# Probabilities handed to fp32r tiles by DMA before their transposes, a new order inside a stream step, and branch projections chained to the stream's fill

## The chip, the cores and the metric

The kernel runs on one core of a Trainium2 chip (trn2). The metric is the device time of one execution in microseconds. The kernel before takes 1494.45 us, the median of three runs (1493.89 to 1494.85).

## The reference

One encoder layer is applied to two groups of requests with the same weights: `prompt` (1024 tokens) and `sample` (512 tokens), both 1024 wide, each with 256 memory tokens.

```
h = rms_norm(x, ln_pre);  z = h @ w_in            # split into nine fields
pool_out  = multiscale_pool(pool_in) * pool_scale
attn_out  = softmax(q k^T / 8) v                  # 8 query heads, 2 key heads, rotary q and k
cross_out = softmax(xq mk^T / sqrt(128)) mv       # 4 heads, 256 memory tokens
branches  = (pool_out * silu(pool_gate), attn_out * silu(attn_gate), cross_out * silu(x_gate))
merged    = sum_n sigmoid(merge_logits_n + b_n) * (branches[n] @ w_branch[n])
y         = x + rms_norm(merged @ w_out, ln_post)
```

Everything is fp32.

## The kernel before

**Arithmetic.** TensorE works on fp32r tiles. Where a product needs more precision, an operand is split into a high part (a copy by ScalarE, line 165) and a low part (a subtraction by VectorE, line 162), and `mm3` (line 132) makes three products of one. All matrix products are recorded at line 126 (`mm`), all transposes at line 130 (`tr`); so one looks at tiles, not lines, to tell them apart. A transpose takes `ident` (fp32) or `identr` (fp32r) as its second operand; in the profile these show as `A<-ident,u` and `B<-identr,u`.

**Tiles.** In SBUF: `u` (128 x 1024, 7 buffers), `med` (128 x 2048, 14), `hu` (128 x 512, 8), `raw` (weights as loaded, 3), `whi`/`wlo` (split weights, 2 each). In PSUM: `A` (two tiles of two banks) and `B` (four tiles of one bank). Intermediate fields go to DRAM scratch and come back (`q`, `xq`, `x_gate`, `attn_gate`, `merge`, `br0` to `br2`). All DMAs are issued by SyncE (SP).

**Stages.** The memory keys and values and the normalised prompt; the prompt's input products (`products`, a scheme with seven products for eight); the first of the sample's input products; then the *stream*; then the branch projections and output products of the three blocks of 512 tokens.

**The stream (lines 888 to 897).** It runs 92 units: 64 of prompt self-attention (`attention`: one 128-token block and one head each), 4 + 4 of prompt cross-attention (`cross`), 16 of sample self-attention (`pairs_of`) and 4 of sample cross-attention. A unit has four parts:

- `ahead`: loads queries two steps early.
- `scores`: query by key products into an `A` tile; VectorE reduces the row maximum (line 782), ScalarE takes the exponential out of PSUM into a `u` tile p (line 784), VectorE the reciprocal of the sum, GpSimd scales p (line 786). Lines 844 to 851 and 927 to 935 are the same for pairs and cross units.
- `turn`: eight 128 x 128 transposes of p into another `A` tile; ScalarE and VectorE split it into `med` tiles.
- `values`: products of the values with the turned probabilities into a `B` tile; `gated` (line 874) or the end of `cross` multiplies by the gate and stores to `br1` or `br2`.

Step i of the stream emits scores of unit i, turn of unit i - 2 (`LAG`), values of unit i - 4 (`LAG + VLAG`). After each of these three parts it yields an amount of TensorE time, and `weave` (line 108) spends that on the *fill*: the rest of the sample's input products (`plain`, 16 pairs of weight tiles), in pieces of twelve products. The price of a product in this planner is its columns over 2.4 ns; of a transpose 107 ns with `ident` and 56 with `identr`, which counts only for transposes in the fill. A unit owes 2560 (cross: 3410) x `SHARE` 0.66 ns per step. Where the fill is spent, the stream goes on alone. After the stream comes what is left of the fill, then `branches(0, sc, merged)`: for three branches, load (`from_scratch`), split, and eight products of twelve matmuls each (`merge`, line 981).

The program order is only a priority: the compiler's scheduler places each engine's instructions in a fixed order by priority and by when their operands and buffers are expected, so an instruction can be pulled ahead. `tc.high_priority` raises some (reductions, splits, evacuations). Engines then run their orders strictly, and wait by semaphore.

Of the kernel before, what the change touches and what calls it, by code (L numbers as in the profile page):

```python
# [61 lines left out]
def encoder_kernel(ctx: ExitStack, tc, wt, xs, xts, mt, cols, rows, rope, edge, ys):  # L62
# [41 lines left out]
    def run(g):  # L104
        for _ in g:
            pass
# [641 lines left out]
    def from_scratch(field, bs, dt=F32):  # L748
# [3 lines left out]
            load(t[:, c * BLK:(c + 1) * BLK], field[c][:, bs])  # L752
        return t

    def attention(b, sc, kt, vt):

        bs = slice(b * BLK, (b + 1) * BLK)
        qd, gd, out = sc["q"], sc["attn_gate"], sc["br1"]
        nch = KC
        units = [(jp, hd, j) for jp in range(TT // 2) for hd in range(NH) for j in range(2)]  # L760
        state = {}

        def ahead(i):
            jp, hd, j = units[i]
            if hd == 0 and j == 0:
                t = M()
                for x in range(2):
                    load(t[:, x * D:(x + 1) * D].bitcast(F32), qd[b * TT + jp * 2 + x][:])
                state["q", jp] = t

        def scores(i):
            jp, hd, j = units[i]
            g = hd // (NH // NG)
            q = state["q", jp][:, j * D + hd * P:j * D + (hd + 1) * P]
            a = A()
            for n in range(2):
                ns = slice(n * 512, n * 512 + 512)
                mm(a[:, ns], q, kt[g][0][:, ns], start=True, stop=False)
                mm(a[:, ns], q, kt[g][1][:, ns], start=False, stop=True)
            mx, sm, rc = S(1), S(1), S(1)  # L780
            with tc.high_priority(PMAX):
                v.reduce_max(mx[:], a[:], axis=AX.X, negate=True)  # L782
                p = U()
                act.activation(p, a[:], AF.Exp, bias=mx[:], accum_out=sm[:])  # L784
            v.reciprocal(rc[:], sm[:])  # L785
            pool.tensor_scalar(p, p, rc[:], 1.0, op0=ALU.mult, op1=ALU.mult)  # L786
            state[i] = p

        def turn(i):
            jp, hd, j = units[i]  # L790
            p = state.pop(i)
            if j == 0:
                state["pt", i // 2] = M()[:], M()[:]
            pv = [t.rearrange("p (c j n) -> p c j n", c=nch, j=2) for t in state["pt", i // 2]]
            tp = A()
            for c in range(nch):
                tr(tp[:, c * P:(c + 1) * P], p[:, c * P:(c + 1) * P], ident)
            tv = tp[:].rearrange("p (c n) -> p c n", c=nch)
            with tc.high_priority(PTURN):
                split(pv[0][:, :, j], pv[1][:, :, j], tv)  # L800

        def values(i):

            jp, hd, j = units[i]
            g = hd // (NH // NG)
            if j == 0:
                state["o"] = B()
            o, pts = state["o"], state["pt", i // 2]
            for c in range(j * nch // 2, (j + 1) * nch // 2):
                for s in range(2):  # L810
                    mm(o[:, :256], vt[:, c, g].rearrange("p s d -> p (s d)"), pts[s][:, c * 256:(c + 1) * 256],
                       start=(c == 0 and s == 0), stop=(c == nch - 1 and s == 1))
            if j == 0:
                return
            del state["pt", i // 2]
            gated(state, jp, hd, o, gd, out, b)

        return [(ahead, scores, turn, values, i, 2560) for i in range(len(units))]

    def pairs_of(sc, kt, vt):  # L820

# [30 lines left out]
            state[i] = p  # L852

        def turn(i):
            p, tp, pt = state[i], A(), M()
            for c in range(4):
                for j in range(2):
                    tr(tp[:, c * 256 + j * P:c * 256 + (j + 1) * P], p[:, j * BLK + c * P:j * BLK + (c + 1) * P], ident)
            with tc.high_priority(PTURN):
                split(pt[:, :D], pt[:, D:], tp[:])  # L860
            state[i] = pt

        def values(i):
# [8 lines left out]
        return [(ahead, scores, turn, values, i, 2560) for i in range(len(units))]  # L872

    def gated(state, jp, hd, o, gd, out, b):
        r = slice((hd % 2) * 64, (hd % 2) * 64 + 64)
        c, cs = hd // 2, slice(b * BLK + jp * 256, b * BLK + jp * 256 + 256)
        if hd % 2 == 0:
            state["ot"] = HU(), HU()
            load(state["ot"][1][:, :256], gd[c][:, cs])
        ot, gt = state["ot"]  # L880
        with tc.high_priority(EVAC):
            act.activation(ot[r, :256], o[64:128, :256], AF.Copy)
            v.tensor_tensor(ot[r, :256], o[0:64, :256], ot[r, :256], op=ALU.add)
        if hd % 2:
            pool.tensor_tensor(ot[:, :256], ot[:, :256], gt[:, :256], op=ALU.mult)
            nc.sync.dma_start(out[c][:, cs], ot[:, :256])

    def stream(units):

        n = len(units)  # L890
        for i in range(-2, n + LAG + VLAG):
            more = units[min(max(i, 0), n - 1)][5] * SHARE / 3
            for k, lag in enumerate((-2, 0, LAG, LAG + VLAG)):
                if 0 <= i - lag < n:
                    units[i - lag][k](units[i - lag][4])
                if k > 0 and i >= 0:
                    yield more

    def cross(b, sc, mkd, mvd):

# [36 lines left out]

        def turn(c):
            p = state[c]
            tp = A()  # L940
            for m in range(2):
                for t in range(TT):
                    tr(tp[:, m * 512 + t * P:m * 512 + (t + 1) * P], p[:, t * 256 + m * P:t * 256 + (m + 1) * P], ident)
            pt = M()
            split(pt[:, 0:1024], pt[:, 1024:2048], tp[:])
            state[c] = pt

        def values(c):
            pt, mv = state.pop(c), state["mv"]
            o = B()  # L950
            for m in range(2):
                s = slice(m * 512 + c * XHD, m * 512 + (c + 1) * XHD)
                mm3(o[:], (mv[0][:, s], mv[1][:, s]), (pt[:, m * 512:(m + 1) * 512], pt[:, 1024 + m * 512:1024 + (m + 1) * 512]), m == 0, m == 1)
            g = HU()
            load(g[:], gd[c][:, bs])
            with tc.high_priority(EVAC):
                v.tensor_tensor(g[:], o[:], g[:], op=ALU.mult)
            nc.sync.dma_start(out[c][:, bs], g[:])

        return [(ahead, scores, turn, values, c, 3410) for c in range(NXH)]  # L960

    def branch_parts(field, bs):
        t = from_scratch(field, bs)
# [153 lines left out]

LAG, VLAG, SHARE, LOOK, WAIT = 2, 2, 0.66, 1, 6  # L1120

AHEAD, EVAC, PMAX, PTURN, LATER = 120, 200, 150, 150, 200

# [89 lines left out]
```

## Time and profile before

The profiled execution took 1496.65 us; the span from first to last instruction is 1494.8 us, and the rest lies around it. Times of stages are windows of that span.

| stage | window, us | length | PE busy | ScalarE busy | clock | DMA share |
|---|---|---|---|---|---|---|
| memory, normalisation | 0 to 75 | 75 | 63.00 | 39.42 | 0.95 | 0.67 |
| prompt input products | 75 to 660 | 585 | 577.24 | 264.42 | 0.99 | 0.34 |
| sample input products, first part | 660 to 692 | 32 | 31.43 | 10.94 | 1.00 | 0.44 |
| stream with the fill | 692 to 1157 | 465 | 453.43 | 288.03 | 0.99 | 0.38 |
| branches, first prompt block | 1157 to 1225 | 68 | 68.00 | 20.26 | 0.97 | 0.71 |
| the other blocks and outputs | 1225 to 1495 | 270 | 262.91 | 86.50 | 1.00 | 0.57 |

PE is TensorE's products, PEld its weight loads (which overlap the products), DVE VectorE, ACT ScalarE, POOL GpSimd, SP SyncE. A row of a group gives line, engine, operation, tile out and tiles in, shapes, the count, then busy time in us and mean ns of one, then the idle time before them and what ended it. A row of the timeline gives start, length, engine, line and operation; "x8" means eight instructions merged, and a bracket is idle time before it with its releaser. Products of TensorE are pipelined and the recorded ends are modelled, so the distance between starts is the cost of one, not its length. A row of the stage view gives window, length, then busy time with count of PE, PEld, DVE, ACT and POOL, then the granted clock, the share of the DMA engines' time and GB/s.

### The profile page before, as it was taken

What the parts mean: (1) busy time and instruction counts of PE and PEld (TensorE: products, weight loads), DVE (VectorE), ACT (ScalarE), POOL (GpSimd) and SP (SyncE); (2) the same over time, 40 slices, a digit from 0 to 9 for tenths busy, and PEclk for the clock granted to TensorE, in tenths of its full rate; (3) what the DMA queues carried; (4) which work ended last, traced back from release to release, by engine and by line L of the source; (5) the groups of instructions that cost most, each with busy time, mean ns of one, the idle gap of its engine ahead of it and who ended that gap; (6) DMA issues with size and microseconds to landing.
All of it is one profiled execution on the core that took longest, in us unless ns stands there. A gap on an engine that the chain in (4) does not pass through costs nothing.

```text
span 1494.8 us, 19564 instructions
## 1 busy us (share of the span) xinstructions
PE 1456.0 (97%) x7264; PEld 1210.1 (81%) x7264; DVE 976.5 (65%) x1215; ACT 709.6 (47%) x1083; POOL 273.3 (18%) x286
## 2 busy tenths in 40 slices
PE   7979999999999999999999999999998999999998
PEld 5768888888888888887888888888886888888887
DVE  6996586666648564747767666676775664764764
ACT  6444444544434545434656556566675233323332
POOL 1000020110000000301222222234232150250241
PEclk9989999999999999999999999999999999999999
DMA  7513233332422434344222223165446844954952
GB/s 277 172 47 106 85 114 125 108 132 66 129 92 78 158 133 128 102 150 148 64 96 80 91 68 106 58 219 173 155 155 214 286 148 132 347 193 140 336 163 84
DMA packets 88174, 211.37 MB, mean 141 GB/s; under 512 B 9872, under 2 KB 19216, under 8 KB 87312
## 3 DMA queue, kind: packets, MB, share of 16 engines
q1 hardware_dynamic: 88080, 210.14, 42.7%
q8 instruction: 57, 0.93, 0.3%
q14 instruction: 37, 0.30, 0.1%
HBM read 155.57 MB, written 54.53 MB: 141 GB/s over the span
## 4 chain that ended last, share of the span: by engine, by line
PE 85%; DMA 4%; DVE 4%; ACT 4%; issue 2%; SPq 1%; POOL 0%; DVEq 0%; POOLq 0%; ACTq 0%
PE B L126 66%; PE A L126 14%; PE A L130 5%; ACT u L784 1%; DVE s L782 1%; ACT whi L165 1%; DMA raw<-wt 1%; DVE wlo L162 1%; PE B L130 1%; DMA hu<-xq 1%; ACT med L165 1%; SPq L139 1%; DMA u<-x_prompt 0%; DMA hu<-merge 0%; DMA hu<-x_gate 0%
## 5 line engine op out<-in xcount | busy, mean ns | idle before, releaser
L126 PE MATMUL B<-med,whi 128*128 128x512 f32 x2776 | 871.2, 394 | 15.8 <-ACT med L165 15.8
L126 PEld LDWEIGHTS B<-med,whi 128*128 128x128 f32 x2776 | 515.8, 189 | 122.2 <-ACT med L165 17.5
L126 PE MATMUL B<-med,wlo 128*128 128x512 f32 x1388 | 544.1, 392 | 0.6 <-DVE wlo L162 0.6
L126 PEld LDWEIGHTS B<-med,wlo 128*128 128x128 f32 x1388 | 261.9, 189 | 56.6 <-DVE wlo L162 1.7
L162 DVE TENSOR_TENSOR wlo<-raw,whi 128x1024 fp32r<-128x1024 f32 (+1 forms) x169 | 213.3, 1263 | 141.6 <-ACT whi L165 140.7
L165 ACT ACTIVATE whi<-raw 128x1024 fp32r<-128x1024 f32 (+1 forms) x169 | 167.5, 991 | 288.5 <-PE B L126 198.3
L165 ACT ACTIVATE med<-A 128x1024 fp32r<-128x1024 f32 x92 | 94.3, 1025 | 108.4 <-PE A L130 108.2
L162 DVE TENSOR_TENSOR med<-A,med 128x1024 fp32r<-128x1024 f32 (+1 forms) x93 | 113.0, 1215 | 42.0 <-ACT med L165 40.8
L187 POOL TENSOR_SCALAR s<-s 128x16 f32<-128x16 f32 (+3 forms) x17 | 6.9, 404 | 669.0 <-DVE s L556 333.2
L786 POOL TENSOR_SCALAR u<-u,s 128x1024 f32<-128x1024 f32 x64 | 72.1, 1127 | 251.3 <-DVE s L785 219.1
L130 PE MATMUL A<-ident,u 128*128 128x128 f32 x784 | 102.8, 273 | 0.9 <-DVE med L162 0.2
L130 PEld LDWEIGHTS A<-ident,u 128*128 128x128 f32 x784 | 90.1, 140 | 16.3 <-issue 5.2
L998 POOL TENSOR_TENSOR med<-med,hu 128x512 f32<-128x512 f32 x48 | 77.0, 1617 | 142.3 <-DVE hu L996 142.2
L782 DVE TENSOR_REDUCE s<-A 128x1 f32<-128x1024 f32 x64 | 78.1, 1220 | 32.9 <-PE A L126 11.3
L126 PE MATMUL A<-kt,med 128*128 128x512 f32 x320 | 91.9, 409 | 2.7 <-ACT u L784 1.2
L126 PE MATMUL A<-whi,med 128*128 128x512 f32 (+1 forms) x320 | 92.4, 368 | 0.2 <-ACT hu L1027 0.2
L784 ACT ACTIVATE u<-A,s 128x1024 f32<-128x1024 f32 x64 | 71.3, 1114 | 38.4 <-DVE s L782 38.0
L165 ACT ACTIVATE whi<-sum 128x1024 fp32r<-128x1024 f32 x50 | 53.1, 1062 | 65.6 <-PE B L126 63.7
L162 DVE TENSOR_TENSOR med<-med,med 128x1024 fp32r<-128x1024 f32 (+1 forms) x50 | 55.8, 1127 | 38.1 <-ACT med L165 34.2
L165 ACT ACTIVATE med<-med 128x1024 fp32r<-128x1024 f32 (+1 forms) x44 | 44.2, 1017 | 74.8 <-POOL med L998 36.2
L162 DVE TENSOR_TENSOR wlo<-sum,whi 128x1024 fp32r<-128x1024 f32 x50 | 61.1, 1221 | 23.3 <-ACT whi L165 22.4
L126 PE MATMUL B<-med,vt 128*128 128x256 f32 x512 | 75.9, 287 | 0.4 <-ACT med L165 0.4
(179 smaller groups left out, 1610.4 us busy)
## 6 DMA issues: line engine op xcount, KB each, us to landing
raw<-wt SPq DMA_DIRECT2D x168, 512.0 KB, 3.7
merge<-hu SPq DMA_DIRECT2D x72, 256.0 KB, 2.0
hu<-merge SPq DMA_DIRECT2D x72, 256.0 KB, 5.2
med<-br SPq DMA_DIRECT2D x36, 256.0 KB, 5.6
q<-hu SPq DMA_DIRECT2D x24, 256.0 KB, 2.6
br<-hu SPq DMA_DIRECT2D x24, 256.0 KB, 2.3
med<-q SPq DMA_DIRECT2D x12, 512.0 KB, 5.0
med<-xt_prompt SPq DMA_DIRECT2D x4, 1024.0 KB, 13.2
```

The source lines that it names most:

```text
L126: pe.matmul(out, l, r, **k)
L130: pe.transpose(out, x, i[:])
L139: return nc.sync.dma_start(out, src)
L162: v.tensor_tensor(out, x, hi.bitcast(F32), op=ALU.subtract)
L165: act.activation(hi, x, AF.Copy)
L187: pool.tensor_scalar(ss, ss, EPS, 1.0, op0=ALU.add, op1=ALU.mult)
L782: v.reduce_max(mx[:], a[:], axis=AX.X, negate=True)
L784: act.activation(p, a[:], AF.Exp, bias=mx[:], accum_out=sm[:])
L786: pool.tensor_scalar(p, p, rc[:], 1.0, op0=ALU.mult, op1=ALU.mult)
L998: pool.tensor_tensor(at, at, sg[:], op=ALU.add)
```

## The change

- A new last part of each unit, `hand`, allocates another `u` tile of type fp32r and copies the scaled probabilities into it by a DMA that ScalarE issues. It runs at the end of the step after the unit's scores.
- `turn` transposes that copy with `identr` into an `A` tile of type fp32r, which is then read as fp32.
- Within a step the order becomes scores, values, turn, hand; `LAG` goes from 2 to 3, so turn comes three steps after the scores, values five.
- The gated outputs of attention and cross units are no longer stored where they are made: they are listed in `finished`, and stored by SP at the end of the following step.
- `branches(0, sc, merged)` is chained to the fill, so that when the sample's input products are spent inside the stream, branch projections follow; what is left of both runs after the stream.

The diff, without the two further `turn` functions (in `pairs_of` and `cross`) that change in the same way:

```
+    def handed(p):
+        t = U(F32R)
+        act.dma_start(t.bitcast(F32), p)
+        return t
+
+    def hand_on(state):
+        def hand(i):
+            state[i] = handed(state[i])
+        return hand
...
-            tp = A()
+            tp = A(F32R)
             for c in range(nch):
-                tr(tp[:, c * P:(c + 1) * P], p[:, c * P:(c + 1) * P], ident)
-            tv = tp[:].rearrange("p (c n) -> p c n", c=nch)
+                tr(tp[:, c * P:(c + 1) * P], p[:, c * P:(c + 1) * P], identr)
+            tv = tp[:].bitcast(F32).rearrange("p (c n) -> p c n", c=nch)
...
-        return [(ahead, scores, turn, values, i, 2560) for i in range(len(units))]
+        return [(ahead, scores, turn, values, hand_on(state), i, 2560) for i in range(len(units))]
...
-            nc.sync.dma_start(out[c][:, cs], ot[:, :256])
+            finished.append((out[c][:, cs], ot[:, :256]))
+
+    finished = []
...
-            more = units[min(max(i, 0), n - 1)][5] * SHARE / 3
-            for k, lag in enumerate((-2, 0, LAG, LAG + VLAG)):
+            more = units[min(max(i, 0), n - 1)][6] * SHARE / 3
+            late = finished[:]
+            finished.clear()
+            for k, lag in ((0, -2), (1, 0), (3, LAG + VLAG), (2, LAG), (4, 1)):
                 if 0 <= i - lag < n:
-                    units[i - lag][k](units[i - lag][4])
-                if k > 0 and i >= 0:
+                    units[i - lag][k](units[i - lag][5])
+                if 0 < k < 4 and i >= 0:
                     yield more
+            for out, x in late:
+                nc.sync.dma_start(out, x)
+        for out, x in finished:
+            nc.sync.dma_start(out, x)
...
-            nc.sync.dma_start(out[c][:, bs], g[:])
-
+            finished.append((out[c][:, bs], g[:]))
...
+    fill = chain(fill, branches(0, sc, merged))
     weave(stream(units), fill)
     run(fill)
-    run(branches(0, sc, merged))
...
-LAG, VLAG, SHARE, LOOK, WAIT = 2, 2, 0.66, 1, 6
+LAG, VLAG, SHARE, LOOK, WAIT = 3, 2, 0.66, 1, 6
```

More of the change, by code (lines that the diff above doesn't have):

```diff
@@ L870, in values @@
             gated(state, jp, hd, o, gd, out, 0)
-        return [(ahead, scores, turn, values, i, 2560) for i in range(len(units))]
+        return [(ahead, scores, turn, values, hand_on(state), i, 2560) for i in range(len(units))]
     def gated(state, jp, hd, o, gd, out, b):
@@ L939, in turn @@
             p = state[c]
-            tp = A()
+            tp = A(F32R)
             for m in range(2):
                 for t in range(TT):
-                    tr(tp[:, m * 512 + t * P:m * 512 + (t + 1) * P], p[:, t * 256 + m * P:t * 256 + (m + 1) * P], ident)
+                    tr(tp[:, m * 512 + t * P:m * 512 + (t + 1) * P], p[:, t * 256 + m * P:t * 256 + (m + 1) * P], identr)
             pt = M()
-            split(pt[:, 0:1024], pt[:, 1024:2048], tp[:])
+            split(pt[:, 0:1024], pt[:, 1024:2048], tp[:].bitcast(F32))
             state[c] = pt
@@ L957, in values @@
                 v.tensor_tensor(g[:], o[:], g[:], op=ALU.mult)
-            nc.sync.dma_start(out[c][:, bs], g[:])
-        return [(ahead, scores, turn, values, c, 3410) for c in range(NXH)]
+            finished.append((out[c][:, bs], g[:]))
+        return [(ahead, scores, turn, values, hand_on(state), c, 3410) for c in range(NXH)]
     def branch_parts(field, bs):
```

6 lines of the change are left out of this document (3 added, 3 removed).

## The prediction

> **What bounds the kernel now.** I read the page first, then the stages, then the PE groups, waits and single rows of the stage that the change touches.
>
> ```profile
> span 1494.8 us, 19564 instructions
> PE 1456.0 (97%) x7264; PEld 1210.1 (81%) x7264; DVE 976.5 (65%) x1215; ACT 709.6 (47%) x1083; POOL 273.3 (18%) x286
> PE 85%; DMA 4%; DVE 4%; ACT 4%; issue 2%; SPq 1%; POOL 0%; DVEq 0%; POOLq 0%; ACTq 0%
> ```
>
> TensorE is busy for 97% of the span and carries 85% of the chain that ended last, so time is won by taking work off TensorE or by filling its holes, and not by making another engine faster. The profiled execution took 1496.65 us (span 1494.8); the median of the runs shown is 1494.45, so I subtract 2.2 us at the end.
>
> The change touches one stage, the stream of attention units, which by the stages (columns: window, length, busy of PE, PEld, DVE, ACT, POOL, clock, DMA share, GB/s) lasts from about 692 to 1157 us:
>
> ```profile
> 805.00:985.00 180.00, 177.56 (x1054) 148.94 (x1053) 118.07 (x143) 107.24 (x155) 49.31 (x47) 1.00 0.29 95
> 1100.00:1144.00 44.00, 43.64 (x279) 38.32 (x278) 31.94 (x42) 34.09 (x77) 18.36 (x30) 1.00 0.60 191
> 1144.00:1157.00 13.00, 5.92 (x26) 4.11 (x23) 6.10 (x7) 2.12 (x3) 0.00 (x0) 0.77 0.93 297
> 692.00:1157.00 465.00, 453.43 (x2680) 384.20 (x2680) 316.88 (x392) 288.03 (x506) 139.77 (x168) 0.99 0.38 123
> ```
>
> There are two kinds of stage in it. Up to 1144 TensorE is full (177.56 of 180). In the last 13 us it does 5.92 us of work, and the granted clock falls to 0.77. Inside the full part the holes are small, and the waits of the weight loads in 692 to 1157 name them (total us, times, longest):
>
> ```profile
> PEld A L126 <- ACT u L784: 11.5, 29, 0.8
> PEld B L126 <- ACT med L165: 8.8, 5, 7.5
> ```
>
> The first is the scores of a unit waiting for a PSUM tile that the exponential of an earlier unit still reads; the second is nearly all the hole at the end (one wait of 7.5).
>
> **Transposes.** 92 units (64 attention, 16 pairs, 12 cross) turn their probabilities with 8 transposes each, 736 in all. They now read fp32; afterwards fp32r. The trace has both forms, since the key and query tails already turn fp32r tiles:
>
> ```profile
> L130 PE MATMUL A<-ident,u 128*128 128x128 f32 x736 | 95.6, 273 | 0.9 <-DVE med L162 0.2
> L130 PE MATMUL B<-identr,u 128*128 128x128 f32 x96 | 11.1, 239 | 0.2 <-DVE u L162 0.2
> ```
>
> ```profile
> 205.09 0.39 PE L126 MATMUL B<-med,wlo 128*128 128x512 f32 x1
> 205.32 0.46 PE L130 MATMUL B<-identr,u 128*128 128x128 f32 x4
> ...
> 206.15 0.40 PE L126 MATMUL B<-med,wlo 128*128 128x512 f32 x1
> 206.38 0.62 PE L126 MATMUL B<-med,whi 128*128 128x512 f32 x2
> 206.84 0.39 PE L126 MATMUL B<-med,wlo 128*128 128x512 f32 x1
> ...
> 623.90 0.80 PE L130 MATMUL B<-identr,med 128*128 128x128 f32 x8
> 624.55 1.06 PE L130 MATMUL A<-ident,med 128*128 128x128 f32 x8
> 625.37 0.71 PE L126 MATMUL B<-med,whi 128*128 128x512 f32 x2
> 625.92 0.40 PE L126 MATMUL B<-med,wlo 128*128 128x512 f32 x1
> ```
>
> Durations overlap, so I price by starts. The fp32 bursts are busy 95.6/92 = 1.039 us each; less the last one's 0.273, over seven gaps, that is 0.1095 us apiece, 0.876 for eight. At 623.90 eight fp32r and eight fp32 transposes stand back to back: from 623.90 to 625.92 is 2.02 us; two 512-column products take 0.46 (206.38 to 206.84), so the sixteen take 1.56, and the fp32r eight 1.56 - 0.876 = 0.684, or 85.5 ns apiece. The bound on one side is the group of four: 205.09 to 206.15 is 1.06; three 512-column products take 0.69 (206.15 to 206.84), so four transposes cost 0.37, 93 ns apiece. On the other side stands the bare spacing within the four, (0.46 - 0.239)/3 = 74 ns. Savings over 736: 12.1 us at 93, 17.6 at 85.5 (0.192 x 92 bursts of eight), 26.1 at 74. I take 17.6, the row with eight in a run, as in the stream.
>
> The Trainium skill ("TensorE: Matmul & The Clock Gate", Back-to-back issue gap) gives about 81 ns for a 128-column product in a stream with weight loads and 56 for the isolated gap, the figure that the kernel's own planner uses; by 81 the estimate would be a saving of 21 us, by 56 one of 39. The row of eight (85.5) agrees with the first and speaks against the second.
>
> **The hole at the end.** The rows (SP's queue, ACT, PE):
>
> ```profile
> 1133.78 0.87 SPq L139 DMA_DIRECT2D u<-x_prompt  x2
> 1146.23 0.43 SPq L139 DMA_DIRECT2D med<-br  x1
> 1154.51 1.06 ACT L165 ACTIVATE med<-med 128x1024 fp32r<-128x1024 f32 x1 [9.00 <-DMA med<-br]
> 1155.62 2.06 PE L126 MATMUL B<-med,whi 128*128 128x512 f32 x3 [7.05 <-ACT med L165]
> 1161.31 0.40 PE L126 MATMUL B<-med,wlo 128*128 128x512 f32 x1
> ```
>
> The branch projections need the pooled branch loaded and split; its load goes out at 1146.23, and the first product runs at 1155.62. TensorE idles 13.0 - 5.92 = 7.1 us, and the next 12 products, 1155.62 to 1161.31, take 5.7 us where 12 x 0.23 = 2.8 is usual: 2.9 more, at the lowered clock. Together 10.0. Now the planner: a step owes the fill 2560 x 0.66 = 1690 ns (3410 x 0.66 = 2251 in cross steps). Over 80 x 1.690 + 12 x 2.251 and four more cross steps at the end that is 171.2 us; the fill holds 32 products of 24 matmuls at 213.3 ns, 163.8. So it runs dry some 7 us before the stream ends. With one step more (lag 3) the stream owes 173.4, and the chained branch work gets 9.6 us: nearly four products of 12 matmuls, placed among the last turns and values, with their load asked for correspondingly earlier. The ends are 0 and 10.0 saved. A load of a still later part of the program went out at 1133.78, so SP was not what held the branch load, more likely a free med tile, and this the change doesn't add. I take 6.
>
> **The copies.** 92 copies of 512 KB from u to u, issued by ScalarE. No such copy is in the trace. The rows for its price are the issue on SP and the landing of transfers of its size:
>
> ```profile
> 902.33 0.42 SPq L139 DMA_DIRECT2D hu<-attn_gate  x1
> 902.72 1.21 DVE L782 TENSOR_REDUCE s<-A 128x1 f32<-128x1024 f32 x1
> 904.03 1.12 ACT L784 ACTIVATE u<-A,s 128x1024 f32<-128x1024 f32 x1 [0.25 <-DVE s L782]
> 905.28 1.19 PE L126 MATMUL A<-kt,med 128*128 128x512 f32 x4 [0.18 <-ACT u L784]
> 905.63 1.13 POOL L786 TENSOR_SCALAR u<-u,s 128x1024 f32<-128x1024 f32 x1 [3.90 <-DVE s L785]
> 909.15 1.19 PE L126 MATMUL A<-kt,med 128*128 128x512 f32 x4
> ```
>
> ```profile
> raw<-wt SPq DMA_DIRECT2D x168, 512.0 KB, 3.7
> y_prompt<-u SPq DMA_DIRECT2D x8, 512.0 KB, 7.3
> ```
>
> ScalarE: 92 x 0.42 = 39 us of queue time on top of 288.0, so 70% of 465 instead of 62%. Queued behind each issue are the next exponentials (which free the PSUM tile for the scores), the high halves of turned tiles and of weights. If TensorE's 11.5 us of waits on the exponential grow with ScalarE's load, that is 11.5 x 39/288 = 1.6 us; if every issue stood ahead of an exponential that TensorE waits for, 39. In the other direction, putting the transposes last takes the turned tile's copy from in front of the exponential, and at most the 11.5 go away. I take 3 lost, near the proportional row, because the issue itself seldom waits: POOL has the probabilities ready at 906.76, 4.0 us after the reduction began, and the copy stands at the end of the following step, a good step after the scores.
>
> The landing is hidden by lag 3: the copy of unit i is issued at the end of step i+1, and its transposes are the third part of step i+3. With steps of 4.5 us that leaves one whole step and the scores, values and two fills of the next, about 3 us: 7.5 us, against 3.7 to 7.3 in the rows. Cover gone, it costs what the slow rival below says.
>
> **Edits at nothing.** Attention and cross outputs are stored a step later from SP; this keeps an hu tile longer but takes a waiting store from in front of loads. It is covered as long as eight hu tiles suffice; if not, an evacuation is late and TensorE waits, which is part of the 3. Lag 3 adds a step at the end with no work of its own. Values before transposes changes who is next, not how much there is.
>
> **Sum.** -17.6 - 6 + 3 = -20.6 us; 1496.65 - 20.6 = 1476.05 in the profiled execution, less 2.2: 1474.
>
> **The rivals.** *The loop of scores takes the saving.* A PSUM tile comes free only after reduction and exponential: 905.28 to 909.15, 3.87 us from scores to scores in a step with little fill. The mean step of the long stretch is still longer, which speaks against; but fill comes in whole products, so about every third step has none, and with 0.42 us of issue in front of the exponential the loop is 4.29, close to the step that is left. Then the transposes' gain becomes waits for ACT u, and what remains is 6 - 3: 1494.45 - 3 = 1491. That fp32r transposes into the A tiles run no faster gives the same time; the rows at 623.90 speak against it.
>
> *More is won.* The waits of 11.5 us go away with the new order, or transposes cost 74 ns (8.5 us more): about 10 us beyond the forecast, 1464. For it speaks that the wait of the scores is a matter of order; against it, that ScalarE gets busier.
>
> *The copies land late, slower than before.* The mechanism is one: a transpose waits for its copy, in order, with everything behind it on TensorE. It decides where the landing passes 7.5 us, and since about 1.6 steps lie between issue and use, each us over it lengthens a step by 0.6. The place is the cross units and their neighbours, some 24 steps, where the DMA share is 0.60 already. By the page
>
> ```profile
> q1 hardware_dynamic: 88080, 210.14, 42.7%
> ```
>
> moved 210.14 MB in 0.427 x 1494.8 = 638 us of all engines, 329 GB/s, so a copy of 0.52 MB is 1.6 us of all engines; in a step of about 5 us that adds 0.3, to 0.9. At a landing of 9 us the 24 steps give back 24 x 0.6 x 1.5 = 21.6 and nothing is won; at 11 they cost 50, and the time is 1474 + 50 = 1524. Against it: most of the stream (0.29 share) has room, and the tiles of the u ring, seven for p, its copy and the cross queries, are enough outside the cross units.
>
> The Trainium skill ("DMA: Bandwidth & Descriptors", Issuing engines are not separate DMA queues) says that transfers issued from different engines share the same 16 DMA engines, so that issuing on ScalarE saves only issue time on SP. That speaks for this rival; no run so far shows two issuing queues side by side.
>
> **How the numbers follow.** A change under 0.2%, about 3 us, cannot be told from none. Forecast 0.53, own range 1467 to 1483 (transposes 12 to 18 us, the end 3 to 10, ScalarE 1 to 6); the scores' loop 0.17, around 1491 and so half within 0.2%; more won 0.15; late copies 0.15. The range 1460 to 1491 takes in the forecast, the better case and two thirds of the loop case, 0.8. Faster 0.53 + 0.15 + 0.10 = 0.78; same 0.07; slower 0.15.
>
> **What would show it.** Right: transposes with identr in the stream, x8 busy about 0.8 us; the branch's first products before 1144, no wait of 7 us on med; the stream with its branch products shorter by 20 us; ACT u waits near 11 to 15. The loop: waits of scores on ACT u of 20 us and more, with PE less than 97% busy in 805 to 985. Late copies: PE waiting for DMA u<-u, and landings over 7.5 us in the list of transfers. The forecast is wrong if transposes stay at 109 ns, or if the hole at the end keeps its place.

## The result, and the profile after

The changed kernel takes 1514.51 us (median of four runs, 1510.76 to 1515.53), against 1494.44 before (median of the runs beside it): a ratio of 1.013, 95% interval 1.0118 to 1.0142. It is 20 us slower where 20 us faster was forecast. The profiled execution took 1515.53 us, with a span of 1513.7.

The page of the changed kernel, its span, busy times and the engines' shares of the chain that ended last:

```profile
span 1513.7 us, 19687 instructions
...
PE 1451.6 (96%) x7264; PEld 1199.9 (79%) x7264; DVE 970.4 (64%) x1215; ACT 710.6 (47%) x1083; POOL 277.8 (18%) x286
...
PE 27%; DMA 2%; DVE 2%; ACT 1%; issue 1%; POOL 1%; SPq 0%; DVEq 0%; ACTq 0%; POOLq 0%
```

TensorE is busy for 4 us less than before, and the span is 19 us longer: it was made to wait, 62 us in all instead of 39. (The chain is followed back only a third of the way here, so its shares can't be set against those of before.) The stages of the changed kernel, in the columns of the stage view, show where:

```profile
692.00:805.00 113.00, 105.82 (x597) 88.03 (x598) 72.74 (x92) 60.63 (x89) 28.86 (x27) 0.95 0.52 186
805.00:985.00 180.00, 168.93 (x1004) 138.78 (x1002) 112.33 (x141) 106.51 (x153) 51.76 (x45) 0.98 0.51 184
1144.00:1157.00 13.00, 11.85 (x80) 10.64 (x81) 9.23 (x12) 10.26 (x32) 5.69 (x10) 1.00 0.42 137
692.00:1157.00 465.00, 440.57 (x2629) 367.30 (x2630) 302.60 (x380) 282.79 (x499) 139.51 (x164) 0.98 0.60 211
```

From 805 to 985, with attention units alone, TensorE has 11.1 us of holes instead of 2.4 and gets 1004 products and transposes done instead of 1054, though the eight transposes of each step have become shorter; in the first 113 us the clock is 0.95. The first cross unit's scores start at 1009.3 us instead of 992.6, the last products of the kernel at 1506.9 instead of 1488.5: of 18.4 us, 16.7 are lost up to the end of the 64 attention steps. Three further views: the first waits of the weight loads from 692 to 1157 us (total, times, longest), the group of the transposes, and the copies:

```profile
PEld B L126 <- ACT med L165: 12.3, 23, 1.3
PEld A L130 <- ACT u L795: 11.0, 14, 1.2
PEld B L126 <- DVE med L162: 8.2, 14, 1.0
...
PEld A L126 <- ACT u L795: 4.4, 8, 2.1
```

```profile
L130 PE MATMUL A<-identr,u 128*128 128x128 f32 x736 | 76.7, 247 | 20.7 <-DMA u<-u 10.3 <-ACT u L795 5.5 <-issue 3.2
```

```profile
u<-u ACTq DMA_DIRECT2D x92, 512.0 KB, 3.2
```

The transposes did become cheaper: 76.7 us of recorded time instead of 95.6. The copies land in 3.2 us (median), far inside the 7.5 us of cover; the 10.3 us for which transposes waited for a copy are three waits, of 0.91 us at 1029.6 and of 5.03 and 4.34 us at the last two cross units. But the waits for the exponential (now line 795) have gone over from the scores to the transposes, and a new kind stands beside them, the values waiting for the split of the turned tile (L165, L162): of the 12.3 us, 9.8 stand in front of values, and all of the 8.2; before it was 1.4 us.

One step of the changed kernel shows how. In the timeline (start, length, engine, line):

```profile
907.79 0.80 PE L130 MATMUL A<-identr,u 128*128 128x128 f32 x8
908.42 1.16 PE L126 MATMUL A<-kt,med 128*128 128x512 f32 x4
908.62 1.03 ACT L165 ACTIVATE med<-A 128x1024 fp32r<-128x1024 f32 x1 [1.65 <-PE A L130]
909.42 1.10 PE L126 MATMUL B<-med,vt 128*128 128x256 f32 x8
909.67 1.23 DVE L793 TENSOR_REDUCE s<-A 128x1 f32<-128x1024 f32 x1 [2.51 <-PE A L126]
...
910.82 1.22 DVE L162 TENSOR_TENSOR med<-A,med 128x1024 fp32r<-128x1024 f32 x1
911.00 1.12 ACT L795 ACTIVATE u<-A,s 128x1024 f32<-128x1024 f32 x1
...
912.25 0.88 PE L130 MATMUL A<-identr,u 128*128 128x128 f32 x8 [0.80 <-ACT u L795]
912.97 0.47 PE L126 MATMUL A<-kt,med 128*128 128x512 f32 x1
```

The transposes at 907.79 and the scores of the next unit at 908.42 follow each other, and each needs one of the two `A` tiles in PSUM. The turned tile is held until its low half is done (910.82 + 1.22 = 912.04, 4.25 us), which on VectorE has to stand behind the reduction of 909.67; the scores' tile until the exponential has read it (911.00 + 1.12 = 912.12, 3.70 us). So both come free at once. TensorE has the values and four products of the fill meanwhile, and then stands for 0.80 us, since the transposes come next. By these rows a unit holds the two tiles for 7.95 us, so that no step with such holds can take less than some 4.0; the 64 steps took 4.69 us each before and 4.96 after. With so little room it matters which user comes next. In the order before, scores stand directly in front of transposes in 54 of 80 steps, and TensorE has hardly a hole: then the next user is the scores, which only need their own tile back, 3.87 us on (the prediction's rows), and the turned tile has until the transposes after them. This reading of one step is an argument; the experiments test it.

### The profile page after: what moved, and what is told of

It is laid out like the page before. It is cut to its first block, busy times and chain, and to the rows that moved or that the text cites. A ratio compares the mean times of both kernels' runs of the same rounds, so it can differ in the third digit from the quotient of the medians.

```text
span 1513.7 us, 19687 instructions
## 1 busy us (share of the span) xinstructions
PE 1451.6 (96%) x7264; PEld 1199.9 (79%) x7264; DVE 970.4 (64%) x1215; ACT 710.6 (47%) x1083; POOL 277.8 (18%) x286
## 5 line engine op out<-in xcount | busy, mean ns | idle before, releaser
L165 ACT ACTIVATE whi<-raw 128x1024 fp32r<-128x1024 f32 (+1 forms) x169 | 167.3, 990 | 296.4 <-PE B L126 201.5
L162 DVE TENSOR_TENSOR wlo<-raw,whi 128x1024 fp32r<-128x1024 f32 (+1 forms) x169 | 209.2, 1239 | 134.6 <-ACT whi L165 133.8
L162 DVE TENSOR_TENSOR med<-A,med 128x1024 fp32r<-128x1024 f32 (+1 forms) x93 | 112.9, 1215 | 30.7 <-ACT med L165 29.3
L165 ACT ACTIVATE med<-A 128x1024 fp32r<-128x1024 f32 x92 | 94.3, 1026 | 76.4 <-PE A L130 76.2
L130 PEld LDWEIGHTS A<-identr,u 128*128 128x128 f32 x736 | 70.8, 141 | 34.4 <-issue 16.0
L130 PE MATMUL A<-identr,u 128*128 128x128 f32 x736 | 76.7, 247 | 20.7 <-DMA u<-u 10.3
L126 PE MATMUL B<-med,vt 128*128 128x256 f32 x512 | 81.1, 289 | 8.2 <-ACT med L165 4.5
L126 PEld LDWEIGHTS B<-med,vt 128*128 128x128 f32 x512 | 70.5, 190 | 21.9 <-ACT med L165 9.7
L165 ACT ACTIVATE whi<-sum 128x1024 fp32r<-128x1024 f32 x50 | 53.0, 1061 | 66.0 <-PE B L126 63.0
L162 DVE TENSOR_TENSOR med<-med,med 128x1024 fp32r<-128x1024 f32 (+1 forms) x50 | 55.3, 1115 | 43.6 <-ACT med L165 39.8
L165 ACT ACTIVATE med<-med 128x1024 fp32r<-128x1024 f32 (+1 forms) x44 | 44.2, 1017 | 79.0 <-POOL med L1017 40.6
```

Of the source, the lines that this page charges most:

```text
L126: pe.matmul(out, l, r, **k)
L130: pe.transpose(out, x, i[:])
L162: v.tensor_tensor(out, x, hi.bitcast(F32), op=ALU.subtract)
L165: act.activation(hi, x, AF.Copy)
```

## The experiments

In the first eight runs the expectations name four theories: ORDER (the new order inside a step costs the time), COPY (the copies do), LAG (three steps of lag), END (the chain and the late stores).

### Undoing one part of the changed kernel

The order inside a step (a_old_order):

```
-            for k, lag in ((0, -2), (1, 0), (3, LAG + VLAG), (2, LAG), (4, 1)):
+            for k, lag in ((0, -2), (1, 0), (2, LAG), (3, LAG + VLAG), (4, 1)):
```

> The changed kernel with one thing undone: within a step turn comes before values again (scores, turn, values, copy); lag 3, copies, chained branches and late stores stay. Theory ORDER (transposes last stand next to the scores of the next step on TensorE, so both PSUM tiles A are filled in one burst and the next burst waits for reduction and exponential of this one, a loop of 4.4 us and more): most of the 20 us comes back and the cheaper transposes show, 1480 to 1495 us. Theory COPY (the copies on ScalarE's queue and in the DMA engines delay exponentials and transposes): still 1508 to 1516. Theory LAG (a longer distance ties up buffers): the same, 1508 to 1516.

Measured 1495.89 us, 1.0013 of before (1.0003 to 1.0023). Undoing the order gives back 18.6 of the 20 us, as ORDER has it; but the time is 0.9 above its range, and the gain of the cheaper transposes doesn't show.

The chain (a_no_chain):

```
-    fill = chain(fill, branches(0, sc, merged))
     weave(stream(units), fill)
     run(fill)
+    run(branches(0, sc, merged))
```

> The changed kernel with the branch projections after the stream again, not chained to the fill. Theory END (the chained branches only move the hole of 10 us: their loads and weights crowd the last copies, for which TensorE waits 5.0 and 4.3 us at 1157 to 1168): 1505 to 1510. If the chain is worth what was forecast, 6 us, it becomes slower: 1518 to 1522. ORDER and COPY leave this open: within 4 us of 1514.

Measured 1512.33 (1.0115; 1.0096 to 1.0133). The stores where they were made (a_no_defer):

```
-            finished.append((out[c][:, cs], ot[:, :256]))
+            nc.sync.dma_start(out[c][:, cs], ot[:, :256])
```

> The changed kernel with the gated outputs stored where they are made, not one step later. ORDER and COPY: within 3 us of 1514. If the late stores are at fault (hu tiles held a step longer, branch inputs of the chain stored late): 1500 to 1508.

Measured 1512.62 (1.0116; 1.009 to 1.0142). Each is within 2.2 us of the changed kernel, and on the faster side, so neither edit gained anything there: END falls. Without copies, with fp32 transposes as before (a_no_copy):

```
-        return [(ahead, scores, turn, values, hand_on(state), i, 2560) for i in range(len(units))]
+        return [(ahead, scores, turn, values, lambda i: None, i, 2560) for i in range(len(units))]
...
-                tr(tp[:, c * P:(c + 1) * P], p[:, c * P:(c + 1) * P], identr)
+                tr(tp[:, c * P:(c + 1) * P], p[:, c * P:(c + 1) * P], ident)
```

> The changed kernel without the copies: fp32 transposes straight from the probabilities with the fp32 identity, as before; order, lag 3, late stores and chained branches stay. ORDER: still slow, and slower by dearer transposes where TensorE is the bound: 1510 to 1530. COPY: 1490 to 1498, near the kernel before.

Measured 1506.0 (1.007; 1.0052 to 1.0088): in the new order, copies and cheaper transposes together lose 8.5 us instead of gaining. The time lies between the ranges of ORDER and COPY and bears out neither alone.

### Making one part alone in the kernel before

The order alone, lag 2 (b_order):

```
-            for k, lag in enumerate((-2, 0, LAG, LAG + VLAG)):
+            for k, lag in ((0, -2), (1, 0), (3, LAG + VLAG), (2, LAG)):
```

> The kernel before with the new order alone (scores, values, turn), lag 2. ORDER: 1508 to 1520, since the transposes now stand next to the scores of the following step. COPY: 1492 to 1498.

Measured 1508.57 (1.0088; 1.007 to 1.0105): 14.1 us lost with no other edit. Lag 3 alone (b_lag3):

```
-LAG, VLAG, SHARE, LOOK, WAIT = 2, 2, 0.66, 1, 6
+LAG, VLAG, SHARE, LOOK, WAIT = 3, 2, 0.66, 1, 6
```

> The kernel before with lag 3 alone. ORDER and COPY: 1492 to 1497, one more step at the end. LAG (tiles tied up longer): 1500 to 1512.

Measured 1492.74 (0.9988; 0.9978 to 0.9997). The chain alone (b_chain):

```
+    fill = chain(fill, branches(0, sc, merged))
     weave(stream(units), fill)
     run(fill)
-    run(branches(0, sc, merged))
```

> The kernel before with the branch projections chained to the fill, alone; some 7 us of branch work may then stand inside the stream's end. If the forecast's 6 us hold: 1486 to 1490. END (the hole only moves): 1492 to 1497.

Measured 1492.81 (0.9988; 0.9979 to 0.9997): 1.6 us, where 6 were forecast. Copies from ScalarE, fp32r transposes and lag 3 in the old order, that is the changed kernel with the diffs of a_old_order, a_no_chain and a_no_defer together (b_copies):

> The kernel before with the copies and fp32r transposes alone, and the lag of 3 that they need; order scores, turn, values, copy; stores and branches as before. Forecast's sum for this part: 1494 - 17.6 + 3 = 1480. ORDER: 1477 to 1490. COPY: 1505 to 1515.

Measured 1494.33 (0.9993; 0.9982 to 1.0004). ORDER stands as the main cause, but here it missed: by the forecast's sum some 14 us should have been won, and nothing was. A second cause was open.

### Where the cheaper transposes' gain went

Three kernels share lag 3 and the old order. The first (c_round) needs no copy: ScalarE's exponential and GpSimd's scaling write the probabilities into fp32r tiles themselves.

```
-                p = U()
+                p = U(F32R)
...
-            pool.tensor_scalar(p, p, rc[:], 1.0, op0=ALU.mult, op1=ALU.mult)
+            pool.tensor_scalar(p, p.bitcast(F32), rc[:], 1.0, op0=ALU.mult, op1=ALU.mult)
```

> The kernel before with three steps of lag, where the exponential and the scaling on GpSimd write the probabilities as fp32r (one tile, rounded where fp32 was kept), and the transposes are fp32r; no copies, old order, no chain. So it measures the cheaper transposes by themselves, against 1492.7 of lag 3 alone. PAID (the transposes save about 17 us and the copies use it up): 1474 to 1479. LOOP (TensorE can't use the saving, since reduction, exponential and PSUM tiles set the pace once the transposes are short): 1488 to 1494, with more waits of the scores on ACT u than in the kernel before. Between them, 1480 to 1488, both have a part.

The second copies from ScalarE's queue into fp32 tiles and keeps the fp32 transposes (c_copy_f32):

```
-        t = U(F32R)
-        act.dma_start(t.bitcast(F32), p)
+        t = U()
+        act.dma_start(t, p)
```

> The kernel before with three steps of lag and the 92 copies from ScalarE's queue, but into fp32 tiles with fp32 transposes: the copies by themselves, against 1492.7. PAID: 1503 to 1510, about as much as cheaper transposes would save. LOOP: 1492 to 1496, the copies cost only what their issue puts in front of exponentials.

The third is b_copies with another queue (c_copy_sp):

```
-        act.dma_start(t.bitcast(F32), p)
+        nc.sync.dma_start(t.bitcast(F32), p)
```

> Copies and fp32r transposes in the old order as in the run of the copies alone (1494.3), but issued from SP in place of ScalarE. PAID, and by the issue on ScalarE: 1480 to 1487. PAID, and by the landing (copy late, or its tile missing): 1494 or slower, up to 1505, since SP's issues wait in order behind loads. LOOP: 1491 to 1495.

Measured: c_round 1477.98 (0.9885; 0.9871 to 0.99), c_copy_f32 1508.78 (1.0088; 1.0071 to 1.0106), c_copy_sp 1475.65 (0.9874; 0.9859 to 0.9889). PAID holds in the first two; in the third the time is 4 us below its range. LOOP falls in all three. Cheaper transposes are worth 1492.7 - 1478.0 = 14.8 us; copies from ScalarE's queue cost 1508.8 - 1492.7 = 16.0; and the same copies from SP cost nothing that shows beside c_round. The stage from 805 to 985 us, of b_copies and then of c_copy_sp:

```profile
805.00:985.00 180.00, 174.17 (x1076) 146.18 (x1075) 125.27 (x149) 112.74 (x163) 50.32 (x48) 0.99 0.58 208
```

```profile
805.00:985.00 180.00, 179.06 (x1107) 150.53 (x1106) 123.57 (x153) 114.78 (x174) 50.89 (x49) 1.00 0.61 213
```

The DMA share is the same (0.58, 0.61), and so is the landing: 92 copies from SP, 3.2 us.

```profile
u<-u SPq DMA_DIRECT2D x92, 512.0 KB, 3.2
```

The Trainium skill ("DMA: Bandwidth & Descriptors", Issuing engines are not separate DMA queues) says that the issuing engine changes only who spends the time to issue, usually little. For the transfers the rows agree (3.2 and 3.2); the 18.7 us between the two kernels must lie elsewhere.

c_round with the edit of b_chain (c_round_chain):

> As the run with rounding on GpSimd, and the branch projections chained onto the fill: the two edits that gained or cost nothing, together. PAID: 1471 to 1478. LOOP: 1485 to 1492.

Measured 1473.56 (median of three runs, 1473.06 to 1477.32; 0.9864; 0.9844 to 0.9884), 4.4 us below c_round, with intervals that overlap.

### ScalarE's time, or the order that the scheduler makes

With the copies in another queue the scheduler also places other instructions differently. TensorE's order in parts of the attention steps (S scores, T transposes, V values, F fill, with their number; not a profile's lines):

```
before and c_copy_sp   S4 T8 V8 F6 S4 T8 F6 V8 S4 T8 V8 F12
b_copies               S4 F12 T8 S4 F5 V1 F5 T8 V7 S4 V8 T8 S4
the changed kernel     S4 F12 T8 S4 F5 V1 F3 T1 V7 T7 S4 V8 T8 S4 V1 F6 V7 T8 S4
```

Two kernels cross the causes. They chain the instructions of each engine, all but the 92 copies, into the order that another kernel has, by edges that bind the order of issue and add no wait (shortened; ORDER stands for a long table):

```
+    for e, order in ORDER:
+        for a, b in zip(order, order[1:]):
+            tc.add_manual_dep(by[b], a, free, reason="order")
```

d_act_pinned is b_copies (copies on ScalarE) in the order of c_copy_sp; d_sp_pinned is c_copy_sp in the order of b_copies. In the traces TensorE, ScalarE, VectorE and GpSimd have, instruction for instruction, the order that was asked for.

> Copies from ScalarE's queue, as in the run of the copies alone (1494.3), but every engine's other instructions are chained into the fixed order that they have in the kernel with the copies on SP (1475.7); the scheduler is free only in where it puts the 92 copies on ScalarE. PLAN (the loss is the order that the scheduler makes when it counts the copies as ScalarE's work): 1475 to 1482. ISSUE (the loss is the time that the issues take on ScalarE at run time, and what stands behind them): 1489 to 1497. In between: both have a share.

> The converse: copies from SP, but every engine's other instructions (SP's other transfers too) chained into the order that they have with the copies on ScalarE. PLAN: 1489 to 1497. ISSUE: 1475 to 1482.

| us | order made for copies on SP | order made for copies on ScalarE |
|---|---|---|
| copies issued by SP | 1475.65 | 1495.06 (1.0003; 0.9994 to 1.0013) |
| copies issued by ScalarE | 1484.67 (0.9939; 0.9919 to 0.9959) | 1494.33 |

In the worse order the queue makes no difference, and SP's copies lose all that they won: PLAN holds for d_sp_pinned. The longest waits are even the same ones. The transposes of the thirtieth attention unit wait in both kernels, after scores and eight values with no fill behind them; first b_copies, then d_sp_pinned:

```profile
835.70 1.08 PE L126 MATMUL A<-kt,med 128*128 128x512 f32 x4
836.62 1.10 PE L126 MATMUL B<-med,vt 128*128 128x256 f32 x8
839.33 0.85 PE L130 MATMUL A<-identr,u 128*128 128x128 f32 x8 [1.61 <-issue]
```

```profile
835.68 1.10 PE L126 MATMUL A<-kt,med 128*128 128x512 f32 x4
836.63 1.10 PE L126 MATMUL B<-med,vt 128*128 128x256 f32 x8
839.46 0.88 PE L130 MATMUL A<-identr,u 128*128 128x128 f32 x8 [1.73 <-ACT u L795]
```

What in that order costs the time is only partly known: from the first scores to those of the first cross unit d_sp_pinned takes 292.1 us and c_copy_sp 284.1, so 8 of the 19 us are lost in the attention steps and the others behind them.

In the better order the queue does cost, 9.0 us, so d_act_pinned falls between its two theories. The stage of 805 to 985 us in d_act_pinned:

```profile
805.00:985.00 180.00, 176.14 (x1078) 147.62 (x1078) 121.11 (x150) 110.19 (x163) 49.73 (x48) 0.99 0.59 211
```

Its runs spread from 1482.3 to 1489.8, and where the copies stand on ScalarE was still the scheduler's choice, so whether another place would save the 9 us stays open.

### The order inside a step, once more

The changed kernel with its copies on SP (d_after_sp; the edit of c_copy_sp):

> The changed kernel with one edit: the copies go out from SP instead of ScalarE. The order inside a step is the new one. ADD (the new order costs its 13 to 19 us by itself): 1488 to 1495, so the change is about as fast as the kernel before or a little faster. ONE CAUSE (the new order only loses because ScalarE is loaded by the copies): 1473 to 1480.

Measured 1518.47 (1.0168; 1.0146 to 1.019). Both expectations fall: what gained 18.7 us in the old order loses 4 here. The same kernel with the old order and the stores where they were, the chain kept (d_sp_chain):

> The changed kernel with the copies on SP, the old order inside a step and the stores where they were: copies, fp32r transposes, three steps of lag and the chained branch projections. From 1475.7, less the 0 to 2.5 us that the chain was worth in other kernels: 1472 to 1476, the fastest so far.

Measured 1479.05 (0.99; 0.9881 to 0.9919): 3 us above the range, and 3.4 us more than without the chain (c_copy_sp).

So the new order has no fixed price. What changes with it can be counted in TensorE's order: the steps, of the 80 of attention and pair units, in which transposes stand directly in front of the next scores, as at 907.79 above. Two kernels were made to test this. e_gap is b_order with all the fill of a step given after turn, so that the new order stays and most of these pairs go. e_round_order is c_round in the new order, with many of them and no copy at all. (The counts in the two expectations, 2, 10, 16 and 20, cover only about the first half of the stream, and so their price of a pair is too high; the whole counts follow below.)

```
-                if k > 0 and i >= 0:
-                    yield more
+                if k == 2 and i >= 0:
+                    yield more * 3
```

> The kernel before with the new order inside a step (scores, values, turn; two steps of lag, no copies), but the whole fill of a step given after turn instead of a third after each part. In the fixed order of TensorE the transposes then stand directly in front of the next scores in 2 of 80 attention steps; in the run of the new order alone (1508.6) it was 10, in the kernel before none, in the changed kernel 16. BACK TO BACK (a step with transposes directly in front of the next scores fills both PSUM tiles at once and TensorE then waits, some 1.4 us each): 1495 to 1500. VALUES (it is the values ahead of the transposes that cost, with fill or without): 1504 to 1511.

> The run with rounding on GpSimd and fp32r transposes (1478.0, no copies, lag 3) with the new order inside a step. In its fixed order TensorE has transposes directly in front of the next scores 20 times, as in the changed kernel with copies on SP (1518.5). BACK TO BACK, at some 1.2 to 1.4 us each: 1500 to 1508. ADD (the new order costs the 13 to 19 us that it cost elsewhere, however often): 1491 to 1497. COPIES (the loss in the changed kernel with copies on SP came from copies, not from order): 1478 to 1485.

Measured: e_gap 1499.16 (1.0033; 1.0021 to 1.0045), e_round_order 1515.77 (1.0139; 1.0119 to 1.0159). In e_gap BACK TO BACK holds: without most of the pairs, 9.4 of the 14.1 us come back. What is left has its rows:

```profile
843.68 1.07 PE L126 MATMUL A<-kt,med 128*128 128x512 f32 x4
844.58 1.10 PE L126 MATMUL B<-med,vt 128*128 128x256 f32 x8
845.52 1.03 PE L130 MATMUL A<-ident,u 128*128 128x128 f32 x8
847.58 1.20 PE L126 MATMUL A<-kt,med 128*128 128x512 f32 x4 [1.03 <-ACT u L784]
```

All five pairs of e_gap stand in steps like this one, without any fill, and at each TensorE waits 1.01 to 1.03 us for the exponential, 5.1 in all, close to the 4.9 lost. From scores to scores it is 3.90 us: this is the loop of the prediction's first rival.

In e_round_order ADD and COPIES fall, since the order costs 37.8 us with no copy in the kernel; BACK TO BACK's 22 to 30 fall short too, by the wrong count. With whole counts:

| kernel | pairs | beside a kernel with none | us lost | per pair |
|---|---|---|---|---|
| e_gap | 5 | before | 4.9 | 0.98 |
| b_order | 15 | before | 14.1 | 0.94 |
| changed kernel | 37 | d_sp_chain | 35.5 | 0.96 |
| d_after_sp | 41 | d_sp_chain | 39.4 | 0.96 |
| e_round_order | 41 | c_round | 37.8 | 0.92 |
| a_no_copy | 17 | b_lag3 | 13.3 | 0.78 |

A pair goes with 0.92 to 0.98 us in the first five and with 0.78 in the sixth, whose neighbour has neither the chain nor the late stores. That is an average, and its evenness is in part chance. TensorE waits longer than 0.2 us at all five pairs of e_gap, at 9 of the 15 of b_order (9.1 us), at 19 of the 37 of the changed kernel (14.6) and at 19 of the 41 of e_round_order (15.7), counting the waits before a pair's transposes or scores and before the next user of an `A` tile; at the other pairs there is no wait of that length. (The last column is worked out after the runs and is no forecast. The changed kernel and d_after_sp store late as well, priced at 2 us at most by a_no_defer, and the changed kernel's copies stand on ScalarE. Pairs don't explain the order of b_copies and d_sp_pinned, which have only 3. Beside a_old_order, which has 3 pairs but the order made for ScalarE's copies, the changed kernel's 34 further pairs cost only 18.6 us: the two bad orders don't add.) The stage from 692 to 985 us, of c_round and then of e_round_order:

```profile
692.00:985.00 293.00, 290.61 (x1784) 244.07 (x1782) 207.38 (x258) 183.45 (x274) 83.94 (x81) 1.00 0.29 96
```

```profile
692.00:985.00 293.00, 273.17 (x1577) 225.72 (x1578) 182.18 (x227) 164.72 (x237) 74.74 (x71) 0.96 0.25 81
```

TensorE stands for 19.8 us instead of 2.4, and the clock is 0.96: 4% of 273 are some 11 us more. Holes (17.4 us more) and clock together are some 28 of the 38 us, in this window alone. The other 10 or so are not accounted for here. So the price of the new order is waits at about half of its pairs and, after some of the longer ones, slower products.

## Why the prediction was wrong, step by step

**The bound** was right: TensorE sets the end, and holes in its stream decide. **The transposes** were right in mechanism and size: 17.6 forecast, 14.8 measured between c_round and b_lag3, inside the bounds of 12.1 and 26.1. **The landing** was right for most of the stream: 7.5 us of cover against a median of 3.2. A copy comes too late three times, by 0.91 us once and by 5.03 and 4.34 at the last two cross units (below). The slow rival, late copies over 24 steps, did not happen.

**The step that failed** is the sentence under the edits at nothing: "Values before transposes changes who is next, not how much there is". That is true of TensorE's work and false of the two PSUM tiles. It cost 18.6 us here, 14.1 alone and 37.8 with cheap transposes and no copies. Where the prediction gave the order a part at all, in the term for the copies and in the rival in which more is won, it was as a gain. The prediction had the row to price it: 3.87 us from scores to scores, set by reduction and exponential. It used that row for the rival of the scores' loop, and there tied it to the fill's lumps and the copies' issue, not to the order. That rival was nearest in kind, but its end (nothing gained, 1491) was on the wrong side of what happened.

**The copies** were mis-sized: 3 us forecast, 16.0 measured in the old order, within the bounds of 1.6 and 39. The forecast counted 0.42 us for each issue and what stands behind it. The runs show instead 9.0 us for the queue in a good order, and, in the order that the scheduler makes when the copies are ScalarE's, 18.7 against the copies on SP. That order was not in the prediction at all.

**The hole at the end** was mis-sized: 6 us forecast. The chain won 1.6 us in the kernel before and 4.4 on c_round, and lost 2.2 in the changed kernel and 3.4 on the copies from SP; the intervals of the last three overlap with those beside them. The window from 1144 to 1157 is full now (11.85 us of work, clock 1.00), but the stream is not over there; the hole has moved behind it, and is larger than the 7.1 us of before:

```profile
1157.00:1175.00 18.00, 8.63 (x42) 7.16 (x41) 8.51 (x9) 6.36 (x8) 3.35 (x5) 0.72 0.93 340
```

The end of the stream in the changed kernel:

```profile
1147.61 8.41 SPq L139 DMA_DIRECT2D raw<-wt  x2
...
1160.99 3.32 SPq L139 DMA_DIRECT2D med<-br  x4
...
1162.85 1.23 PE L130 MATMUL A<-identr,u 128*128 128x128 f32 x8 [5.03 <-DMA u<-u]
...
1166.41 1.06 ACT L165 ACTIVATE med<-med 128x1024 fp32r<-128x1024 f32 x1 [6.03 <-DMA med<-br]
```

Loads of a branch go out only at 1160.99, after two weight loads, whose issue takes 8.41 us of SP's queue, and some smaller transfers, and the transposes of one of the last cross units wait 5.03 us for their copy, with everything behind them on TensorE.

**The signs** that were to show the forecast right partly misled: waits for ACT u came to 11.0 + 4.4 = 15.4 us, close to the 11 to 15 given, but 11.0 of them in front of transposes; the values' waits for splits (9.8 and 8.2) were on no list. "PE less than 97% busy in 805 to 985" was one sign of the loop, and it came true (168.93 of 180 is 94%); the other, scores waiting 20 us for the exponential, did not (4.4).

**Late stores and lag 3** at nothing: right (1.9 us lost, inside the noise of those runs, and 1.7 us won).

The parts, each the difference of two runs, so that the sum must close: 1492.7 with lag 3, less 14.8 for the transposes, plus 16.4 for copies from ScalarE is 1494.3 (b_copies); chain and late stores 1.6, 1495.9 (a_old_order); the order 18.6, 1514.5.

**The version that follows.** Lag 3, old order and copies from SP take 1475.65 us, 1.3% less than the kernel before; fp32r written by GpSimd with the chain takes 1473.56, the same within the intervals. Both are near what the prediction expected of the whole change, 1474.

## What to carry to other kernels

Before pricing a reorder at nothing, count the buffers that the moved instructions hold, and what other work is left between one use of a buffer and the next: where it is shorter than the hold (here 3.7 and 4.25 us), the engine that was never short of work waits. Two users of a ring of two that stand back to back need not cost anything by themselves: scores before transposes, in 54 of 80 steps of the kernel before, left 2.4 us of holes in 180; transposes before scores, in 37 of the changed kernel, left 11.1. An instruction moved to another engine's queue changes what a scheduler counts on that engine, and so the fixed order of all the others; compare the orders first (here 19 us lay between two orders of the same instructions), and cross order and queue before blaming either. Time saved on the bounding engine has to be kept by the order as well: the 14.8 us of the cheaper transposes were there in c_round and gone in e_round_order.

## What the hardware showed that was not expected

A single wait of under 2 us was followed by some 3 us at half the clock. In the changed kernel TensorE stands once for 1.93 us, before the second of these rows:

```profile
707.63 0.79 PE L130 MATMUL A<-identr,u 128*128 128x128 f32 x8
710.35 1.97 PE L126 MATMUL A<-kt,med 128*128 128x512 f32 x4 [1.93 <-ACT u L795]
```

The stage view in slices of one microsecond (the clock is the third number from the end):

```profile
709.00:710.00 1.00, 0.00 (x0) 0.00 (x0) 1.00 (x2) 1.00 (x2) 0.00 (x0) 1.00 0.43 176
710.00:711.00 1.00, 0.65 (x2) 0.56 (x3) 0.64 (x2) 1.00 (x3) 0.21 (x1) 0.74 0.97 361
711.00:712.00 1.00, 1.00 (x4) 0.81 (x3) 0.76 (x1) 0.21 (x1) 0.92 (x1) 0.50 0.87 131
712.00:713.00 1.00, 1.00 (x4) 0.80 (x4) 1.00 (x2) 0.00 (x0) 0.00 (x0) 0.50 0.72 254
713.00:714.00 1.00, 1.00 (x4) 0.77 (x4) 0.60 (x1) 0.04 (x1) 0.00 (x0) 0.55 0.95 356
714.00:715.00 1.00, 1.00 (x8) 0.91 (x7) 0.00 (x0) 1.00 (x2) 0.00 (x0) 1.00 0.16 57
```

After 1.93 us of idling, some 3 us of work run at half speed: the wait costs about 1.5 us more than itself. Not every wait of this kind does it. In e_round_order 1.73 us of waiting before 852.38 were followed by a clock of 0.55 and 0.50; after the same 1.73 us in d_sp_pinned, shown above, it stayed at 1.00:

```profile
839.46:843.00 3.54, 3.42 (x19) 2.52 (x19) 3.10 (x5) 1.29 (x2) 2.88 (x2) 1.00 0.13 42
```

What decides between the two was not tested. The Trainium skill ("TensorE: Matmul & The Clock Gate", HAM oscillation) puts the danger at idle gaps of over some 3.4 us; here a gap of 1.93 us went before the slow stretch. The same page of the Trainium skill (A second HAM failure mode: psum-queue depth-cycling) tells of short idles between groups of products that set the clock swinging when PSUM banks are cycled. The many short waits of e_round_order, with a clock of 0.96 from 692 to 985, agree with that.
